# Fifty small chained transfers on the SP queue of a sliding-window kernel

## The chip, the cores and the metric

The kernel runs on one core of a Trainium2 chip. The metric is the time of one execution on the device in microseconds (us): 193.0 us, the median of three runs (192.89 to 193.47). A profiled execution has in addition a span, from its first to its last instruction; durations below come from that one execution.

The engines named here are ACT (ScalarE), DVE (VectorE), POOL (GpSimd) and SP (SyncE). SP, ACT and POOL issue DMA transfers; 16 DMA engines carry them out. In the profile the DMA queue of SP is q1, that of ACT is q10 and that of POOL is q0.

## The reference

The input `x` has 16 images of 64 channels with 64 x 64 float32 values. Windows of 8 x 8 are cut out at every fourth row and column, 15 x 15 of them, for every image and channel.

```python
n_h = (h - window_size) // stride + 1
n_w = (w - window_size) // stride + 1
for i in range(n_h):
    for j in range(n_w):
        h_start = i * stride
        w_start = j * stride
        result[:, i, j] = x[:, :, h_start:h_start + window_size, w_start:w_start + window_size].copy()
```

Nothing is computed: values are copied, each to about four places. 16.8 MB are read and 59 MB written.

## The kernel before

The whole input is held on the core in one tile `L`. A partition stands for an image, one half of the channels and one quarter of the rows (16 x 2 x 4 = 128 partitions), and holds 32 channels x 16 rows x 64 columns. Lines 49 to 54 load it in 16 transfers of 1 MB, in turn from SP and ACT, eight each. A transfer reuses one of eight completion semaphores, so the second four on each queue wait for the first four to land.

Then windows are copied out of `L` into contiguous buffers, and these are scattered to the output. The work is a list of 60 pairs (j, s), where j is the window's column (15 of them) and s the window's row within the quarter (4 of them). The function `window` does one pair, or one half of its channels. For s = 0 to 2 ACT makes the copy into a buffer `g` (line 111). For s = 3 the window reaches into the next quarter, that is into the next partition: DVE copies the upper half (line 113) and fetches the lower one with a shuffle across partitions (line 114). There are nine buffers `G0` to `G8`, each for one whole pair or two halves, used in turn.

A finished buffer is written in one of two ways:

- Usually POOL issues an indirect DMA, a scatter (line 124): each of the 128 partitions writes one contiguous row, of 8 KB for a whole pair or 4 KB for a half, to the place that an index tile names (`idx`, `idx_last`, and `idx_h`, `idx_hlast` for halves).
- For the last two pairs (`TAIL = 2`, line 115) SP issues plain stores, one for each quarter (line 118): four for the first and three for the second, 256 KB each. These seven are called the tail stores below.

The first twelve pairs (`EARLY`, line 135) begin with the first half of the channels, which has been loaded first; their second halves follow in between later pairs. Then a plain loop runs over the rest (line 146). Before the last two pairs `at` is set back by three buffers (line 148), so that they take buffers that come free early.

The order of the instructions on each engine is that of the program text. A framework adds the waits that data dependences need. The stores to `out` are declared free of dependences on each other (function `free`). On SP, therefore, the program before has eight loads and then seven tail stores, the first of which waits for an ACT copy into its buffer and the fifth for DVE's.

Of the kernel before, what the change touches and what calls it, by code (L numbers as in the profile page):

```python
# [1 line left out]

# [4 lines left out]


@with_exitstack  # L10
def kernel(
    ctx: ExitStack,
    tc: tile.TileContext,
    x: bass.AP,
    window_size: int,
    stride: int,
    out: bass.AP,
):
    nc = tc.nc
    P = nc.NUM_PARTITIONS  # L20

    B, C, H, W = x.shape
    Bo, NH, NW, Co, WSo, WSo2 = out.shape
    WS = int(window_size)
    ST = int(stride)
    assert Bo == B and Co == C and WSo == WS and WSo2 == WS

    f32 = mybir.dt.float32
    i32 = mybir.dt.int32
    ALU = mybir.AluOpType  # L30
    HQ = 4
    CH = P // (B * HQ)
    CL = C // CH
    RB = H // HQ
    NSLOT = RB // ST
    NWIN = NH * NW
    CFREE = CL * WS * WS
    assert HQ == 4 and CH == 2 and WS == 2 * ST

    lpool = ctx.enter_context(tc.tile_pool(name="lpool", bufs=1))  # L40
    ipool = ctx.enter_context(tc.tile_pool(name="ipool", bufs=1))
    gpool = ctx.enter_context(tc.tile_pool(name="gpool", bufs=1))


    L = lpool.tile([P, CL, RB, W], f32)
    x_v = x.rearrange("b (ch cl) (hq r) w -> hq (b ch) cl (r w)", ch=CH, hq=HQ)
    NCH = 4
    cw = CL // NCH
    for k in range(NCH):
        for q in range(HQ):  # L50
            (nc.sync, nc.scalar)[q % 2].dma_start(
                out=L[q::HQ, k * cw : (k + 1) * cw, :, :],
                in_=x_v[q, :, k * cw : (k + 1) * cw, :],
            )


    def itile(name):
        return ipool.tile([P, 1], i32, name=name)

    pi, tb, tq, tc_, idx, idx_last = (itile(n) for n in ("pi", "tb", "tq", "tc", "idx", "idx_last"))  # L60
    nc.gpsimd.iota(pi[:, :], pattern=[[0, 1]], base=0, channel_multiplier=1)  # L61
    nc.vector.tensor_scalar(out=tb[:, :], in0=pi[:, :], scalar1=3, scalar2=None, op0=ALU.logical_shift_right)  # L62
    nc.vector.tensor_scalar(out=tc_[:, :], in0=pi[:, :], scalar1=2, scalar2=1, op0=ALU.logical_shift_right, op1=ALU.bitwise_and)  # L63
    nc.vector.tensor_scalar(out=tq[:, :], in0=pi[:, :], scalar1=HQ - 1, scalar2=None, op0=ALU.bitwise_and)  # L64
    nc.vector.tensor_scalar(out=tb[:, :], in0=tb[:, :], scalar1=float(NWIN * CH), scalar2=None, op0=ALU.mult)  # L65
    nc.vector.tensor_tensor(out=tb[:, :], in0=tb[:, :], in1=tc_[:, :], op=ALU.add)  # L66
    nc.vector.tensor_scalar(out=tc_[:, :], in0=tq[:, :], scalar1=float(NSLOT * NW * CH), scalar2=None, op0=ALU.mult)  # L67
    nc.vector.tensor_tensor(out=idx[:, :], in0=tb[:, :], in1=tc_[:, :], op=ALU.add)  # L68

    nc.vector.tensor_scalar(out=tq[:, :], in0=tq[:, :], scalar1=float(HQ - 1), scalar2=float(2 * B * NWIN * CH), op0=ALU.is_equal, op1=ALU.mult)  # L70
    nc.vector.tensor_tensor(out=idx_last[:, :], in0=idx[:, :], in1=tq[:, :], op=ALU.add)  # L71


    HCL = CL // 2
    idx_h, idx_hlast = itile("idx_h"), itile("idx_hlast")
    for d, e in ((idx_h, idx), (idx_hlast, idx_last)):
        nc.vector.tensor_scalar(out=d[:, :], in0=e[:, :], scalar1=2.0, scalar2=None, op0=ALU.mult)  # L77
    o_v = out.rearrange("b i j (ch cl) r w -> (b i j ch) (cl r w)", ch=CH)
    o_h = out.rearrange("b i j (ch cl) r w -> (b i j ch) (cl r w)", ch=2 * CH)
    nxt = [min(p + 1, 31) for p in range(32)]  # L80

    order = [(j, s) for j in range(NW) for s in range(NSLOT)]


    TAIL, BACK = 2, 3
    o_q = out.rearrange("b i j (ch cl) r w -> i j b ch (cl r w)", ch=CH)

    def free(st):
        tc.declare_no_dep(st.ins, group="stores", reason="each store writes rows of its own")
        tc.add_to_no_dep_group("stores", st.ins)  # L90


    UNITS = 18
    G = [gpool.tile([P, 2 * HCL, WS, WS], f32, name=f"G{n}") for n in range(UNITS // 2)]
    at = 0

    def window(j, s, half):
        nonlocal at
        cols = slice(j * ST, j * ST + WS)
        last = s == NSLOT - 1  # L100
        if half is None:
            n, c0 = 2, 0
            at += at % 2
        else:
            n, c0 = 1, half * HCL
        u = at % UNITS
        at += n
        cs = slice(c0, c0 + n * HCL)
        g = G[u // 2][:, u % 2 * HCL : (u % 2 + n) * HCL, :, :]
        if not last:  # L110
            nc.scalar.copy(out=g, in_=L[:, cs, s * ST : s * ST + WS, cols])  # L111
        else:
            nc.vector.tensor_copy(out=g[:, :, 0:ST, :], in_=L[:, cs, s * ST : RB, cols])  # L113
            nc.vector.stream_shuffle(out=g[:, :, ST:WS, :], in_=L[:, cs, 0:ST, cols], mask=nxt)  # L114
        if (j, s) in order[-TAIL:]:
            g_q = g.rearrange("(m q) c r w -> q m (c r w)", q=HQ)
            for q in range(HQ - 1 if last else HQ):
                free(nc.sync.dma_start(out=o_q[q * NSLOT + s, j], in_=g_q[q]))
            return
        if half is None:  # L120
            o, ix = o_v, (idx_last if last else idx)
        else:
            o, ix = o_h, (idx_hlast if last else idx_h)
        st = nc.gpsimd.indirect_dma_start(  # L124
            out=o,
            out_offset=bass.IndirectOffsetOnAxis(ap=ix[:, 0:1], axis=0),
            in_=g.rearrange("p c r w -> p (c r w)"),
            in_offset=None,
            element_offset=(s * NW + j) * CH * CFREE + (half or 0) * HCL * WS * WS,
            bounds_check=B * NWIN * CH * (1 if half is None else 2) - 1,  # L130
            oob_is_err=False,
        )
        free(st)

    EARLY = 12
    for j, s in order[:EARLY]:
        window(j, s, 0)
    late = list(order[:EARLY])
    rest = list(order[EARLY:])
    while late:  # L140
        for w in late[:2]:
            window(*w, 1)
        for w in rest[:2]:
            window(*w, None)
        late, rest = late[2:], rest[2:]
    for w in rest[:-TAIL]:
        window(*w, None)
    at -= 2 * BACK
    for w in rest[-TAIL:]:
        window(*w, None)  # L150


# [1 line left out]
_INS = ['x', 'window_size', 'stride']  # L154
_OUTS = [((16, 15, 15, 64, 8, 8), 'float32')]

_NUMBERS = {'window_size': 8, 'stride': 4}


# [26 lines left out]
```

## Time and profile before

| What | Value |
|---|---|
| median of three runs | 193.0 us |
| profiled execution | 193.19 us |
| its span | 191.4 us |
| busy: ACT, POOL, DVE | 86.2, 68.0, 30.4 us |
| bytes moved by DMA, mean rate | 75.80 MB, 396 GB/s |
| packets: SP queue, ACT queue, POOL queue | 2512, 2176, 10080 |
| share of the 16 DMA engines: POOL, SP, ACT queue | 73.3%, 13.8%, 11.1% |
| a 1 MB load from SP, issue to landing (median) | 21.1 us |
| a scatter of a whole pair, issue to landing (median) | 18.4 us |
| a tail store of 256 KB, issue to landing (median) | 4.2 us |

Busy times count an engine's own work; issuing a DMA is not counted. The time from issue to landing of a transfer includes its wait behind others, and with several transfers of a queue under way it is far longer than the transfer itself. Where a profile's line gives packets of a queue, a packet is one contiguous row that one DMA engine moves, or a semaphore update of 4 bytes.

### The profile page before, as it was taken

The numbers are of one execution on the slowest core, as the hardware profiler recorded it, in microseconds if no ns is written. First come the engines' busy times: TensorE is split into PE (matmuls) and PEld (weight loads), VectorE is DVE, ScalarE is ACT, GpSimd is POOL, SyncE is SP. The second block draws the span as 40 slices with busy tenths as digits, with TensorE's granted clock in tenths as the row PEclk, the third lists the DMA queues.
The fourth block names the chain that finished last, engine by engine and source line by source line (L and its number), as shares of the span: only waits on it lengthen the run. The fifth ranks groups of instructions, "written<-read, shape, count | busy, mean of one in ns | idle before, by whom it ended". The sixth has DMA issues, their size and how long they took to land.

```text
span 191.4 us, 479 instructions
## 1 busy us (share of the span) xinstructions
DVE 30.4 (16%) x65; ACT 86.2 (45%) x55; POOL 68.0 (36%) x75
## 2 busy tenths in 40 slices
DVE  2000050000232302301221031203030303000030
ACT  0000059400699876364566556565647473300300
POOL 0000028723367666464464343434444444400000
DMA  5999999999999999999999999999999999999785
GB/s 180 419 413 410 410 409 413 416 423 420 417 423 429 423 418 425 407 406 414 410 413 404 414 416 413 404 409 409 411 407 409 411 409 406 416 411 416 325 265 187
DMA packets 14772, 75.80 MB, mean 396 GB/s; under 512 B 2032, under 2 KB 2032, under 8 KB 9008
## 3 DMA queue, kind: packets, MB, share of 16 engines
q0 software_dynamic: 10080, 57.15, 73.3%
q1 hardware_dynamic: 2512, 10.22, 13.8%
q10 hardware_dynamic: 2176, 8.39, 11.1%
q14 instruction: 4, 0.03, 0.0%
HBM read 16.78 MB, written 62.65 MB: 415 GB/s over the span
## 4 chain that ended last, share of the span: by engine, by line
DMA 73%; issue 19%; ACT 2%; POOL 1%; DVE 1%; POOLq 0%; DVEq 0%; PEldq 0%; ACTq 0%
DMA out_dram<-G,idx 60%; DMA out_dram<-G,idx_h 13%; ACT G L111 2%; POOL out_dram L124 1%; DVE G L114 1%; DVE G L113 0%; POOLq L124 0%; POOL pi L61 0%; DVEq L113 0%; PEldq L181 0%; ACTq L111 0%
## 5 line engine op out<-in xcount | busy, mean ns | idle before, releaser
L111 ACT COPY G<-L 128x2048 f32<-128x2048 f32 (+1 forms) x54 | 84.9, 1611 | 69.1 <-DMA out_dram<-G,idx_last 25.1
L124 POOL DMA_INDIRECT out_dram<-G,idx x35 | 33.8, 966 | 45.9 <-DMA out_dram<-G,idx 41.7
L113 DVE COPY G<-L 128x1024 f32<-128x1024 f32 (+1 forms) x18 | 11.1, 614 | 152.1 <-DMA out_dram<-G,idx 76.5
L124 POOL DMA_INDIRECT out_dram<-G,idx_h x18 | 17.4, 964 | 13.9 <-DMA out_dram<-G,idx_hlast 4.8
L114 DVE STREAM_SHUFFLE G<-L 128x1024 f32<-128x1024 f32 (+1 forms) x18 | 19.6, 1091 | 0.0
L124 POOL DMA_INDIRECT out_dram<-G,idx_hlast x6 | 5.9, 989 | 27.8 <-DVE G L114 26.3
L124 POOL DMA_INDIRECT out_dram<-G,idx_last x11 | 10.6, 964 | 10.6 <-DVE G L114 5.8
L111 ACT ACT_TABLE_LOAD x1 | 1.3, 1283 | 25.9 <-DMA L<-in_x_dram 25.9
L62 DVE TENSOR_SCALAR tb<-pi 128x1 int32<-128x1 int32 x1 | 0.2, 154 | 1.0 <-POOL pi L61 1.0
L61 POOL IOTA pi<- 128x1 int32 x1 | 0.1, 119 | 0.4 <-PEq L181 0.4
L114 DVE LOAD_MASK_SELECT G<-L x18 | 0.2, 12 | 0.0
L167 POOL MEMSET const-float32-0.0<- 128x1 f32 x1 | 0.1, 98 | 0.2 <-issue 0.2
L66 DVE CUSTOM_DVE_ANT_0 tb<-tb,tc 128x2 uint16<-128x2 uint16 x1 | 0.2, 160 | 0.0
L68 DVE CUSTOM_DVE_ANT_0 idx<-tb,tc 128x2 uint16<-128x2 uint16 x1 | 0.2, 158 | 0.0
L67 DVE TENSOR_SCALAR tc<-tq 128x1 int32<-128x1 int32 x1 | 0.2, 153 | 0.0
L77 DVE TENSOR_SCALAR idx_hlast<-idx_last 128x1 int32<-128x1 int32 x1 | 0.2, 153 | 0.0
L77 DVE TENSOR_SCALAR idx_h<-idx 128x1 int32<-128x1 int32 x1 | 0.2, 154 | 0.0
L71 DVE CUSTOM_DVE_ANT_0 idx_last<-idx,tq 128x2 uint16<-128x2 uint16 x1 | 0.2, 153 | 0.0
L65 DVE TENSOR_SCALAR tb<-tb 128x1 int32<-128x1 int32 x1 | 0.2, 151 | 0.0
L70 DVE TENSOR_SCALAR tq<-tq 128x1 int32<-128x1 int32 x1 | 0.1, 147 | 0.0
L64 DVE TENSOR_SCALAR tq<-pi 128x1 int32<-128x1 int32 x1 | 0.1, 144 | 0.0
L63 DVE TENSOR_SCALAR tc<-pi 128x1 int32<-128x1 int32 x1 | 0.1, 143 | 0.0
(3 smaller groups left out, 0.3 us busy)
## 6 DMA issues: line engine op xcount, KB each, us to landing
L<-in_x_dram SPq DMA_DIRECT2D x8, 1024.0 KB, 21.1
L<-in_x_dram ACTq DMA_DIRECT2D x8, 1024.0 KB, 19.8
out_dram<-G SPq DMA_DIRECT2D x7, 256.0 KB, 4.2
out_dram<-G,idx POOLq DMA_INDIRECT x35, 18.4
out_dram<-G,idx_h POOLq DMA_INDIRECT x18, 14.1
out_dram<-G,idx_last POOLq DMA_INDIRECT x11, 18.4
out_dram<-G,idx_hlast POOLq DMA_INDIRECT x6, 11.9
```

The source lines that it names most:

```text
L61: nc.gpsimd.iota(pi[:, :], pattern=[[0, 1]], base=0, channel_multiplier=1)
L62: nc.vector.tensor_scalar(out=tb[:, :], in0=pi[:, :], scalar1=3, scalar2=None, op0=ALU.logical_shift_right)
L65: nc.vector.tensor_scalar(out=tb[:, :], in0=tb[:, :], scalar1=float(NWIN * CH), scalar2=None, op0=ALU.mult)
L66: nc.vector.tensor_tensor(out=tb[:, :], in0=tb[:, :], in1=tc_[:, :], op=ALU.add)
L67: nc.vector.tensor_scalar(out=tc_[:, :], in0=tq[:, :], scalar1=float(NSLOT * NW * CH), scalar2=None, op0=ALU.mult)
L68: nc.vector.tensor_tensor(out=idx[:, :], in0=tb[:, :], in1=tc_[:, :], op=ALU.add)
L71: nc.vector.tensor_tensor(out=idx_last[:, :], in0=idx[:, :], in1=tq[:, :], op=ALU.add)
L77: nc.vector.tensor_scalar(out=d[:, :], in0=e[:, :], scalar1=2.0, scalar2=None, op0=ALU.mult)
L111: nc.scalar.copy(out=g, in_=L[:, cs, s * ST : s * ST + WS, cols])
L113: nc.vector.tensor_copy(out=g[:, :, 0:ST, :], in_=L[:, cs, s * ST : RB, cols])
L114: nc.vector.stream_shuffle(out=g[:, :, ST:WS, :], in_=L[:, cs, 0:ST, cols], mask=nxt)
L124: st = nc.gpsimd.indirect_dma_start(out=o, out_offset=bass.IndirectOffsetOnAxis(ap=ix[:, 0:1], axis=0), in_=g.rearrange("p c r w -> p (c r ...
```

## The change

Between the part that treats the early pairs and the loop over the rest, a tile `S` of 128 partitions x 512 B is made, in a pool of its own. Fifty transfers are then issued from SP, each the same: the first 512 B of each of the sixteen images of `x` go to sixteen partitions of `S` (32, 36, ... 92). Nothing reads `S`. Since all fifty write the same place, each one waits until the one before it has landed.

```diff
             window(*w, None)
         late, rest = late[2:], rest[2:]
+
+    spool = ctx.enter_context(tc.tile_pool(name="spool", bufs=1))
+    S = spool.tile([P, 128], f32, name="S")
+    x_s = x.rearrange("b c h w -> b (c h w)")
+    for n in range(50):
+        nc.sync.dma_start(out=S[32:93:4, :], in_=x_s[:, 0:128])
+
     for w in rest[:-TAIL]:
         window(*w, None)
     at -= 2 * BACK
```

On SP the order becomes: eight loads, the fifty transfers, seven tail stores. The instructions of ACT, DVE and POOL stay the same, in the same order.

## The prediction

> **What bounds the kernel now.** I read the 40 slices first, then the chain that ended last, then the waits of SP, then the DMA queues in short windows, and last the trace's packet records themselves (each DMA packet with queue, size, start and duration).
>
> ```profile
> DMA  5999999999999999999999999999999999999785
> ...
> GB/s 180 419 413 410 410 409 413 416 423 420 417 423 429 423 418 425 407 406 414 410 413 404 414 416 413 404 409 409 411 407 409 411 409 406 416 411 416 325 265 187
> ...
> DMA 73%; issue 19%; ACT 2%; POOL 1%; DVE 1%; POOLq 0%; DVEq 0%; PEldq 0%; ACTq 0%
> ```
>
> The 16 DMA engines are full from 5 us to about 177 us at some 412 GB/s; no compute engine is near its limit (ACT 45%). Only the last three slices, from 177 us, have slack. The kernel is bound by bytes, then by a short tail. The SP queue's own instructions and waits:
>
> ```profile
> 0.73 25.68 SPq L51 DMA_DIRECT2D L<-in_x_dram  x8
> 181.14 6.21 SPq L118 DMA_DIRECT2D out_dram<-G  x7
> ```
>
> ```profile
> SPq L118 <- ACT G L111: 154.0, 1, 154.0
> SPq L51 <- DMA L<-in_x_dram: 20.1, 4, 6.6
> ```
>
> SP issues eight loads up to 25.8 us, sleeps 154 us for the last ACT copy, and issues the seven tail stores of L118 from 181.14 us. The last of these lands at 190.4, and the span ends at 191.4. So anything put on SP has 154 us in which it delays no instruction; after that, each us of delay moves the end by a us. The price of a small transfer in a full DMA system is the whole question, so I looked at how the queues share the engines. Three queues were active between 31.6 and 34 us:
>
> ```profile
> q1 hardware_dynamic: 88, 0.36, 36.6%
> q10 hardware_dynamic: 89, 0.36, 36.3%
> q0 software_dynamic: 88, 0.29, 30.3%
> ```
>
> Columns are packets, MB, share of 16 engines. SP (q1), ACT (q10) and POOL (q0) got equal packet counts; in the packet records an engine serves them one packet each in turn. That is for queues that are already filled. A transfer that arrives new fares worse, seen at two places. First the start, between 2.2 and 4.6 us:
>
> ```profile
> q10 hardware_dynamic: 191, 0.78, 95.4%
> ...
> L<-in_x_dram SPq DMA_DIRECT2D x3, 1024.0 KB, 18.3
> L<-in_x_dram ACTq DMA_DIRECT2D x2, 1024.0 KB, 16.9
> ```
>
> SP and ACT issued their first loads together (0.735 and 0.738 us), yet ACT's packets start at 2.23 and run alone, 11 to 20 on an engine, until SP's first at 4.68 us: 2.45 us behind. Second the tail, between 182.4 and 183.3 us:
>
> ```profile
> q1 hardware_dynamic: 16, 0.13, 52.7%
> q0 software_dynamic: 21, 0.17, 45.8%
> ```
>
> The first store (issued 181.14) starts at 182.44 to 182.66 us on the eight engines that had run out of scatters. The eight still busy finish all their scatter packets (up to seven of 8 KB, 309 ns each) and start it only at 183.3 to 184.05 us, without taking turns.
>
> **What the Trainium skill says.** "DMA: Bandwidth & Descriptors", section "Queues, rings and completion order", says that each engine goes round-robin between queue rows and "drains a whole packet" of some 9 to 17 descriptors before it switches. The steady alternation above is finer than that, one 4 KB record each; the two late arrivals look more like it. The same page, "Anatomy of one DMA", prices a transfer at about 2.0 us fixed, most of it the receipt of the last write, fitted for transfers issued from GpSimd; no lone small transfer is in this trace, but the pieces below sum to 2.1 us. Its section on why a DMA increments its semaphore by 16 says that a transfer whose slowest dimension is 16 uses 16 engines, and all must have landed. The trace agrees: each tail store has 16 semaphore landings. So the slowest of 16 engines sets each step.
>
> **The change part by part.** Nothing is removed. Tile S and 50 transfers are added. In the compiled program they stand on SP between the eight loads and the seven stores; ACT, DVE and POOL keep the same instructions in the same order. All 50 write the same rows of S, so each waits for its predecessor's completion; the first eight also wait for the loads that used their semaphores before. It is a chain of round trips, not a stream.
>
> Bytes: 50 x 16 x 512 B = 0.41 MB, at 412 GB/s 1.0 us, plus 800 semaphore packets of 9 ns over 16 engines, 0.45 us. Beside the scatters about two thirds of this counts: 1 us on their end. No compute engine needs S.
>
> Start: transfer 1 is issued after SP's last load (25.8 us) and a load of ACT's that lands at 27.1. It stands in SP's queue behind four loads, the last of which lands at 49.5. So transfer 1 lands at about 49.9, and transfer 2 is issued there. From that issue to the issue of transfer 50 are 48 steps.
>
> Idle step, once the scatters are over: issue to first packet 1.30 us (181.14 to 182.44), 0.3 more for a first packet (8 KB took 616 ns there against 309 in the stream), 512 B 0.02, semaphore packet to landing 0.45 (median of 128 on SP's loads 0.49, in the tail about 0.35), landing to SP's next issue 0.02 (10.44 to 10.457): 2.1 us. Bounds 1.8 (tail values, no extra read time) to 2.4 (the first load took 1.49 us to its first packet).
>
> Loaded step: 1.30, plus the wait behind packets that the engine has already taken in, plus 0.02, plus one 8 KB scatter packet taken in turn ahead of the semaphore packet 0.31, plus 0.47, plus 0.02; without the wait that is 2.12. The wait is the unknown. If arrivals took turns at once it is at most one packet, 0 to 0.31, and the step 2.1 to 2.45. The tail gives 1.6 (184.05 less 182.44, a lower end, since the scatters ran out there). The start gives 2.45. If an engine takes in a number of packets, not of bytes, then 13 of 309 ns are 4.0. I take 2.1, which is 13 packets of 4 KB at 159 ns: the wait is then one of bytes (53 KB an engine). Loaded step 4.2 us; both ends kept: 3.4 to 6.2.
>
> Sum: the scatters end at 184.2 in the packet records, 185.5 with the added traffic. From 49.9 that is 135.6 us, 32.3 loaded steps. The remaining 15.7 take 33 us idle. Transfer 50 is issued at 218.5, the first store at 219.1. From there the tail took 10.25 us before (181.14 to 191.4); its eight busy engines are now free, so I take 9.7. Span 228.8; with the 1.8 us that the profiled execution has around its span (193.19 less 191.4) 230.6. The median of the runs shown is 193.0, 0.2 below the profiled one, inside the rounding. Forecast 231 us.
>
> By the same sum, a loaded step of 3.4 gives 215, 5.0 gives 241, 6.2 gives 252 (260 with the idle step at 2.4); the idle step at 1.8 takes 5 off the forecast. The 154 us sleep covers the chain as long as its step is below (181.14 - 0.6 - 49.9)/48 = 2.72 us: beyond that point the stores wait.
>
> **Rivals.**
> First, *deep queue*: the engine holds a count of packets, and 8 KB ones make the wait 4 us. For: 11 to 20 of ACT's packets ran before SP's first, and the records show packets, not bytes. Against: a scatter's first packet on the busy engines at 31.6 us came 3.2 us after POOL's instruction ended at 28.4, with two queues full, which leaves no room for two counts of 13. 244 to 262 us.
>
> Second, *shallow queue*: arrivals wait hardly a packet or two more than on a free engine, step 2.75 to 3.4. For: the alternation between filled queues is one for one, so a queue never waits long by turn alone. Against: both late arrivals. The first store needed 4.0 us from issue to its last landing (185.16), with a single packet more than a small transfer. 196 to 213 us.
>
> Third, *the other side, absorbed*: the step is below 2.72 us, the chain ends before 181 us in SP's sleep, and the tail starts where it did. Then only the bytes count. Where the scatters' added 1 us is taken up by the slack of the last three slices (half of the engines are done at 180.9 while the rest run to 184.2), the time stays 192.8 to 193.6, not slower; where it lands on the slow half it is 194 to 196. Speaking for it: turns one for one price the step at 2.1 to 2.45. It decides only if the wait of a new arrival is under 0.6 us.
>
> That the change doesn't do what it says: the order on SP and the waits between the 50 are in the compiled program, so I give it nothing.
>
> **How the numbers follow.** Main case (step 3.4 to 5.2) 213 to 244 us, 0.62; deep 0.15; shallow 0.13; absorbed 0.10, of which slower by bytes 0.05, no change 0.03, faster 0.02 (nothing in the profile makes it faster but a chance re-timing of the tail). About 0.3%, 0.6 us, is what a measurement of this kernel tells from no change. Range: 208 to 255 leaves out the fastest part of the shallow case, the absorbed one and the deep case's upper end, together about 0.2. Faster 0.02, same 0.03, slower 0.95.
>
> **What would show it.** SP's row: 50 transfers from 26 us, one after the other, the spacing 4.2 us to about 185 us and 2.1 us after; the stores of L118 at about 219 us, waiting for S and no longer for ACT. POOL, ACT and DVE end within 2 us of where they did. DMA slices full to 185 us, then nearly empty for over 30 us, then 4 to 5 us busy. The scatters' waits unchanged. I am wrong if the spacing beside the scatters is under 2.72 us, if it is the same before and after 185 us, or if the scatters themselves slow by more than 3 us because small packets break their stream.

## The result and the profile after

| | before | after |
|---|---|---|
| median time | 193.09 us (192.89 to 193.47, 4 runs) | 241.43 us (241.21 to 242.09, 4 runs) |
| profiled execution, its span | 193.19, 191.4 us | 241.38, 239.6 us |
| last scatter packet ends | 184.2 us | 184.3 us |
| first tail store issued | 181.1 us | 229.9 us |
| first store to the end of the span | 10.3 us | 9.7 us |

The ratio is 1.2506, 95% interval [1.2475, 1.2538]: slower by 48 us. The forecast was 231 us, slower by 38, in a range of 208 to 255.

The page of the changed kernel, its 40 slices (6 us each): share of the DMA engines and what they moved.

```profile
DMA  6999999999999999999999999999993000000045
...
GB/s 223 419 409 409 410 416 420 421 417 422 422 424 420 410 408 409 412 417 412 414 410 408 409 413 406 412 413 406 416 419 157 4 6 4 4 4 5 5 134 176
```

The copying is as fast as before and as early done. Then follow seven slices, some 42 us, in which the DMA engines move 4 to 6 GB/s, which is one small transfer at a time, and only after them the two slices of the tail stores. The same in the timeline of SP (start, duration, instructions):

```profile
0.73 25.69 SPq L51 DMA_DIRECT2D L<-in_x_dram  x8
27.11 202.77 SPq L151 DMA_DIRECT2D S<-in_x_dram  x50
229.92 4.88 SPq L118 DMA_DIRECT2D out_dram<-G  x7
```

SP's waits show what took the place of its sleep (engine, line, what it waited for: total, times, longest). Before, the tail stores waited 154 us for ACT; that row is gone, and the chain waits for itself, 49 times:

```profile
SPq L151 <- DMA S<-in_x_dram: 173.6, 49, 18.9
SPq L51 <- DMA L<-in_x_dram: 20.1, 4, 6.6
SPq L151 <- DMA L<-in_x_dram: 3.9, 2, 3.3
```

One view has to be read with care. These are two rows of the waits of the other engines:

```profile
DVE G L113 <- DMA S<-in_x_dram: 20.8, 1, 20.8
...
ACT G L111 <- DMA S<-in_x_dram: 13.8, 1, 13.8
```

They look as if DVE and ACT waited for the chain. They don't: nothing reads S. Both wait for the loads of L, and transfer 1 uses the completion semaphore of one of these loads again, so the profile puts its name there. The last load landed at 49.55 us, the two copies began at 49.65 and 49.67, and transfer 1 landed only at 49.88. Before, the same 13.8 us of ACT stood against the load.

The price of a step is read from the transfers that write S, in two windows of the changed kernel: 100 to 175 us, beside the scatters, and 187 to 205 us, with the DMA engines free.

```profile
L151 SPq DMA_DIRECT2D S<-in_x_dram x13: 492/492/493, 99.9 to 169.6; - x13
...
DMA to landing us min/median/max: 5.5/5.7/6.5
```

```profile
L151 SPq DMA_DIRECT2D S<-in_x_dram x10: 492/492/492, 186.8 to 203.4; - x10
...
DMA to landing us min/median/max: 1.8/1.8/1.9
```

From issue to landing the same 8 KB take 5.7 us beside the scatters and 1.8 us alone. A step, from one issue to the next, is hardly longer: from transfer 2, issued at 49.9 us, to transfer 26 at 184.8 there are 24 steps of 5.62 us on average; from there to transfer 50 at 229.4 another 24, of 1.86 us.

Transfer 25, issued at 180.84 us, falls between the two. At that time half of the engines run out of scatters, and the other half have scatters up to 184.3. Its sixteen packets split in the same way: eight start 1.37 to 1.49 us after the issue, as on free engines, and the other eight at 183.90 to 184.29 us, just when the last scatter packets end (183.86 to 184.28). The records name no engine, so the packets are matched by time; the same split of eight and eight is there in e3 and e12. The wait is thus one at the single engine, behind its scatters, and not one of the transfer as a whole.

### The profile page after: what moved, and what is told of

It is laid out like the page before. It is cut to its first block, busy times and chain, and to the rows that moved or that the text cites. A ratio compares the mean times of both kernels' runs of the same rounds, so it can differ in the third digit from the quotient of the medians.

```text
span 239.6 us, 534 instructions
## 1 busy us (share of the span) xinstructions
DVE 30.6 (13%) x65; ACT 86.2 (36%) x55; POOL 68.2 (28%) x75
## 4 chain that ended last, share of the span: by engine, by line
DMA 64%; ACT 5%; issue 4%; POOL 1%; SPq 1%; DVE 1%; POOLq 0%; ACTq 0%; DVEq 0%
DMA out_dram<-G,idx 48%; DMA L<-in_x_dram 9%; DMA out_dram<-G,idx_h 7%; ACT G L111 5%; POOL out_dram L124 1%; SPq L51 1%; ACT L111 1%; DVE G L114 1%; DVE G L113 0%; POOLq L124 0%; ACTq L111 0%; DVEq L113 0%
## 6 DMA issues: line engine op xcount, KB each, us to landing
out_dram<-G,idx_h POOLq DMA_INDIRECT x18, 13.8
```

## The experiments

The main theory: each new transfer waits behind what every DMA engine has already taken in from the scatters; fifty such round trips (from issue to landing) in a chain outlast SP's sleep; and the tail stores stand behind them on SP. Rivals: the cost goes by bytes or by number; it is the latency of reading device memory while it is being written; it is something that grows with the rows of a transfer.

**A shorter chain** (e1_len24).

```diff
-    for n in range(50):
+    for n in range(24):
```

> The chain cut from 50 to 24 transfers. Theory (the chain delays only the tail stores, and only after SP's sleep is used up): transfer 24 is issued at about 175 us, before the last ACT copy ends, so the stores start at 181.1 us as without a chain and the time is 193.0 to 194.3 us. Rival (each small transfer disturbs the scatters by itself): 24 of 50 transfers cost 24/50 of the 48 us, 216 us.

Measured: 193.35 us against 193.13 beside it, ratio 1.0012 [0.9998, 1.0026]. The timeline of SP in this kernel:

```profile
27.18 149.82 SPq L151 DMA_DIRECT2D S<-in_x_dram  x24
181.69 6.16 SPq L118 DMA_DIRECT2D out_dram<-G  x7
```

The 24 transfers take 150 us and cost nothing that can be measured, because SP has nothing else to do until 181 us. The rival of a fixed price for each transfer, 216 us here, falls.

**The same transfers without the chain** (e2_tiles8).

```diff
-    S = spool.tile([P, 128], f32, name="S")
+    S = [spool.tile([P, 128], f32, name=f"S{m}") for m in range(8)]
-        nc.sync.dma_start(out=S[32:93:4, :], in_=x_s[:, 0:128])
+        nc.sync.dma_start(out=S[n % 8][32:93:4, :], in_=x_s[:, 0:128])
```

> All 50 transfers stay, with the same bytes and packets, but go to eight tiles in turn, so that each waits for the eighth before it. Theory (the wait on the one before is what costs): eight round trips run side by side, 50 transfers take some 7 x 5.7 us = 40 us, end near 92 us, and the time is 193.0 to 194.5 us. Rival (fifty more transfers cost by their number or by their bytes in a full system): 235 us or more.

Measured: 194.82 us against 193.13, ratio 1.0086 [1.0054, 1.0118]. All 50 transfers with all their bytes are there, and the 48 us are not: the dependence makes them. What is left is 1.7 us, 0.3 above the expected bound; the prediction had priced bytes and turns at 1.0 to 1.45 us. The chain ended at 100 us, some 8 us later than expected, with the transfers going out every 1.43 us. The expectations of e5 and e6 below read this as a round trip of 8 x 1.43 = 11.5 us. The trace says otherwise. SP's instructions between 70 and 98 us:

```profile
L151 SPq DMA_DIRECT2D S<-in_x_dram x20: 1360/1395/1456, 69.6 to 97.0; - x20
```

The DMA instruction itself takes 1.4 us instead of 0.49, and the next one starts some 44 ns after it. SP's waits in this run have no row for S: it is never held up by the eighth transfer before. The last packet of a transfer starts some 5.9 us after its issue, against 5.03 in the chain, and long before the eighth transfer after it goes out. So the waits overlap, and what sets the pace is SP's issuing; why an instruction takes longer with some four transfers under way stays open.

**Two and three under way** (e5_tiles2, e6_tiles3): the same edit with two tiles (`n % 2`) and three (`n % 3`).

> The 50 transfers go to two tiles in turn: each waits for the second before it, two are under way. If two waits overlap fully, a pair takes 5.7 us, 2.85 each, 47 are done beside the scatters, and transfer 50 is issued at about 186: 197 us. If each transfer under way adds 0.8 us to the round trip, as eight under way (11.5 us for a round trip against 5.7 for one) suggest, a pair takes 6.5, 3.25 each, some 41 are done by 185 and the last is issued at about 191: 203 us. Rival (the engine serves one small transfer of SP's in each 5.7 us, however many are under way): 241 us.

> Three tiles in turn, three under way. By 4.9 + 0.8 us for each one under way a round trip takes 7.3 us, 2.4 us a transfer, under the 2.72 us that SP's sleep allows: the chain ends near 168 us, the stores start where they did, and only the bytes and turns are left, 194.0 to 195.2 us. Rival (depth doesn't matter or the cost goes by number): 230 us or more.

Measured: two tiles 194.27 us (one run, beside 193.39), three tiles 194.69 us, ratio 1.0072 [1.0052, 1.0092]. SP's timeline with two tiles:

```profile
27.35 155.45 SPq L151 DMA_DIRECT2D S<-in_x_dram  x50
182.85 5.05 SPq L118 DMA_DIRECT2D out_dram<-G  x7
```

My estimate that each transfer under way adds 0.8 us was wrong: transfer 3 is issued at 50.1 and transfer 50 at 182.3 us, 23.5 pairs of 5.63 us, so two waits overlap fully. I also counted a step too many, since transfers 1 and 2 both went with the loads. With two under way the chain just fits (the stores start 1.7 us later than before), and nearly the whole loss is gone. With three the last transfer is issued at 138.9 us, where I expected 168.

**Another source** (e3_from_sbuf).

```diff
-        nc.sync.dma_start(out=S[32:93:4, :], in_=x_s[:, 0:128])
+        nc.sync.dma_start(out=S[32:93:4, :], in_=L[32:93:4, 0, 0:2, :].rearrange("p r w -> p (r w)"))
```

> The 50 transfers read 512 B from sixteen partitions of L instead of from x. Theory (the extra 3.2 us of a step beside the scatters are a wait behind scatter packets that each DMA engine has already taken in): the source doesn't matter, the step stays at 5.5 to 5.9 us beside the scatters and 1.7 to 1.9 after them, 239 to 242 us. Rival (the extra is the time that a read from device memory takes while the scatters write there at full rate): the step falls to 2.3 to 2.8 us beside the scatters, the chain fits in SP's sleep, 193 to 196 us.

Measured: 236.38 us. The transfers of this kernel, 100 to 175 us and 187 to 205 us:

```profile
L150 SPq DMA_DIRECT2D S<-L x13: 486/487/487, 99.8 to 169.6; - x13
...
DMA to landing us min/median/max: 5.4/5.7/6.1
```

```profile
L150 SPq DMA_DIRECT2D S<-L x12: 486/487/487, 186.8 to 204.9; - x12
...
DMA to landing us min/median/max: 1.6/1.6/1.6
```

Between 100 and 175 us the step is the same to the hundredth, 5.74 us on average in both kernels; alone it is 0.2 us shorter, which over the 24 idle steps makes the 5 us of difference. (The time lies 2.6 us under the range that I had expected; the idle step of 1.64 us lay just under mine.) Reading device memory is not what makes the loaded step long.

**One row instead of sixteen** (e8_one_row).

```diff
-        nc.sync.dma_start(out=S[32:93:4, :], in_=x_s[:, 0:128])
+        nc.sync.dma_start(out=S[32:33, :], in_=x_s[0:1, 0:128])
```

> Each of the 50 transfers moves one row of 512 B only, on one DMA engine instead of sixteen. Theory (the step is set by the slowest of sixteen engines, each with about the same wait): the median engine's packet came 0.3 us before the last one's beside the scatters and 0.1 us after them, so the step falls to 5.2 to 5.5 us and 1.65 to 1.8 us, 236 to 240 us. Rival (the step's excess grows with the number of engines or rows[...]): under 4 us beside the scatters, under 225 us.

Measured: 220.37 us; the step is 4.96 us beside the scatters (100 to 175 us) and 1.21 alone. SP's instruction, from 100 to 175 us:

```profile
L151 SPq DMA_DIRECT2D S<-in_x_dram x15: 202/202/203, 103.1 to 172.7; - x15
```

The packet records split the time from the issue to the start of the 512 B packet:

| mean | issue to packet, scatters | issue to packet, alone | difference |
|---|---|---|---|
| sixteen rows, median engine | 4.76 us | 1.39 us | 3.37 us |
| one row | 4.31 us | 0.86 us | 3.45 us |

Both sides were off. The rival had named under 225 us, and the time is there, but the loaded step is not under 4 us, and what the scatters add is the same with one engine as with sixteen. What does grow with the rows is the fixed part, which I had expected to fall by 0.1 to 0.2 us and which fell by 0.6. About half of that is the DMA instruction itself, which takes 202 ns on SP for one row and 492 ns for sixteen.

**Is it packets or bytes?** (e4_half_rows, e9 to e11.) First all scatters in halves:

```diff
     for w in rest[:-TAIL]:
-        window(*w, None)
+        window(*w, 0)
+        window(*w, 1)
```

(and the same for the pairs between the late halves).

> All scatters go out as halves, so that their packets are 4 KB and not 8 KB; twice as many, the same bytes. The wait of a new transfer behind scatter packets was 3.25 us with 8 KB packets (10.5 of them). If an engine takes in a fixed number of packets: wait 1.7, step 3.5 to 4.0 us. If it takes in a fixed number of bytes: wait 3.25, step 5.3 to 5.6. If it is between, as steps 2 and 3 of the chain beside 4 KB packets suggest (2.6): step 4.6 to 5.0 us. The time follows from the step, from about 222 (3.8) over 234 (4.8) to 240 us (5.5), if POOL keeps the queue filled with twice as many scatters.

Measured: 223.29 us. The time is no answer, as POOL couldn't keep the queue filled with twice as many scatters: the last scatter packet ended at 197.9 us, not at 184.3. The kernel in windows (after the window's length: busy of DVE, ACT, POOL; clock; DMA share; GB/s):

```profile
50.00:100.00 50.00, 11.82 (x33) 38.27 (x39) 34.89 (x36) 1.00 1.00 400
100.00:150.00 50.00, 10.71 (x30) 28.19 (x27) 33.55 (x34) 1.00 0.91 354
150.00:180.00 30.00, 4.35 (x12) 13.57 (x13) 22.07 (x23) 1.00 0.88 343
```

Where the share falls to 0.9 the step falls to 3.19 us on average (32 steps from 88 us on): a little slack in the queues takes 2.5 us off. But from 59 to 83 us the queue was still full, every scatter packet had 4 KB, and four transfers came then. Their packets took 4.82 us from issue on the median engine, 3.43 over the idle 1.39 (3.2 to 3.9 in the four). Beside 8 KB packets it was 3.37. Divided by a packet's median time, that is some 22 packets of one kind (159 ns each) and 11 of the other (314 ns), and 88 KB of both. A fixed count of 11 packets would have waited 1.7 us here; these four rule it out.

Then the start of the program, where POOL loads L and the chain runs beside it: all loads on POOL, the chain moved ahead, the rows of a load cut by `PIECES` = 1, 2, 4 (with `NK` = 4, 2, 1, so that a load stays at 1 MB).

```diff
+    for k in range(NK):
+        for g in range(PIECES):
+            for q in range(HQ):
+                nc.gpsimd.dma_start(
+                    out=L[q::HQ, ck * k : ck * k + ck, rk * g : rk * g + rk, :],
+                    in_=x_v[q, :, ck * k : ck * k + ck, rk * W * g : rk * W * (g + 1)],
+                )
```

> All sixteen loads of L go on POOL's queue, in packets of 4 KB, and the chain starts on SP beside them, at the start of the program. In the first 40 us each transfer of the chain arrives while every engine has loads of POOL's queued. Wait of its first packet (time from issue, less the 1.28 us of an idle system): if an engine takes in bytes (some 53 to 84 KB), 2.1 to 3.3 us; if it takes in 10 to 13 packets, 1.6 to 2.1 us. This run is the base for the next two.

> The same with the loads in packets of 2 KB, the same bytes in each load. Bytes: the wait stays within 0.4 us of that beside 4 KB packets. Count: it falls to about half of it, some 0.8 to 1.1 us.

> The same with the loads in packets of 1 KB. Bytes: the wait stays within 0.6 us of that beside 4 KB packets (more if such packets move slower). Count: about a quarter of it, some 0.4 to 0.6 us.

Measured: 221.99, 226.76 and 228.07 us; the times also hold the slower loads and the rest of the chain. What was asked for is the wait from 14 to 36 us. From issue to landing, rows of 4 KB (e9):

```profile
DMA to landing us min/median/max: 4.7/4.7/4.8
```

Rows of 2 KB (e10):

```profile
DMA to landing us min/median/max: 5.0/5.0/5.0
```

Rows of 1 KB (e11):

```profile
DMA to landing us min/median/max: 5.3/5.4/5.4
```

The wait doesn't fall with shorter rows; it rises about as much as the loads slow down. On the median engine it is 2.54, 2.74 and 3.09 us over the idle 1.39, with the loads at 411, 388 and 348 GB/s. Times a sixteenth of that rate: 65, 66 and 67 KB. With one reservation: the records show packets of 4 KB in all three, several short rows in one, so these runs vary the rows and the rate and not the packet. They can't tell 66 KB from 16 packets of 4 KB; only the halves above can. Taken together bytes fit and a fixed count does not, but it is not one number of bytes: some 66 KB an engine of loads, some 88 KB of scatters. Why scatters have more of it stays open.

**Another engine for the stores** (e7_stores_on_act).

```diff
-                free(nc.sync.dma_start(out=o_q[q * NSLOT + s, j], in_=g_q[q]))
+                free(nc.scalar.dma_start(out=o_q[q * NSLOT + s, j], in_=g_q[q]))
```

> The seven tail stores are issued by ACT, the chain of 50 stays on SP. Theory (the 48 us are the chain's length plus the stores queued behind it): the stores land by 191 us, the end is the landing of transfer 50 at 231 us, span 232 and time 234 us, so that 7 to 8 of the 48 us go and the rest is the chain itself. Rival (the order on SP alone makes it late, not the chain's length): 193 to 196 us.

Measured: 235.54 us, near the expected 234, since the chain ended at 231 us as forecast. But the stores did not land by 191 us. In the timeline of ACT:

```profile
179.64 1.90 ACT L111 COPY G<-L 128x2048 f32<-128x2048 f32 x1 [14.48 <-DMA out_dram<-G,idx_last]
...
217.53 12.21 ACTq L118 DMA_DIRECT2D out_dram<-G  x7
```

The stores were free of SP's queue and still started 36 us after the copy. In the trace, SP and ACT share eight completion semaphores, used in turn. The first store gets the one of transfer 43 and has to wait for it: transfer 43 was issued at 215.67 us and landed at 217.5. The six others follow transfers 44 to 49 one by one, each within 0.1 us of the landing. So moving the stores to another queue does not free them from the chain here, and how much of the loss is their place behind it on SP was not measured.

**A chain in between** (e12_len32): 32 transfers.

> The chain cut to 32 transfers. By the changed kernel's steps, transfers 2 to 25 take 5.6 us beside the scatters and each later one 1.86: 18 fewer of these, 241.4 - 18 x 1.86 = 208 us, within 1.5. Rival (the cost goes by the number of transfers, 48.3/50 each): 224 us.

Measured: 206.73 us, 1.3 below the 208 of the steps and 17 below the rival's 224. The timeline of SP:

```profile
27.18 169.14 SPq L151 DMA_DIRECT2D S<-in_x_dram  x32
196.36 4.48 SPq L118 DMA_DIRECT2D out_dram<-G  x7
```

By these runs transfers cost nothing measurable up to 24 (e1). Between 32 and 50 they cost a little under 2 us each: (241.43 - 206.73) / 18 is 1.93, and the steps themselves 1.86. The rest is in the tail, which from the first store to the end of the span took 8.5 us here and 9.7 with 50 transfers.

None of the runs is faster than the kernel before.

## Why the prediction was right, and what it had wrong

**Bound and mechanism**: right. The bytes end at 184.3 us as before (184.2), SP's 154 us sleep is used up by the chain (50 transfers against 24, e1 and the changed kernel), and each us after that moves the end (e12). The chain is what costs, not the bytes: with all 50 transfers but more of them under way, 0.9 to 1.7 us are left (e2, e5, e6). I had taken 1 us for bytes and turns; how much of what is left is theirs was not separated, and in e5 later stores are part of it.

**The loaded step** is the term that was mis-sized, and in it the wait:

| term | taken | measured |
|---|---|---|
| issue to first packet, free engines | 1.30 us | 1.28 us |
| wait behind what is taken in, over that | 2.1 us | 3.5 us median engine, 3.75 slowest |
| scatter packet ahead of the semaphore's | 0.31 us | 0.33 us |
| semaphore packet to landing, next issue | 0.49 us | 0.4 us |
| loaded step | 4.2 us | 5.7 us |
| idle step | 2.1 us | 1.86 us |

(The waits of 3.4 us above are over 1.39 us, the median engine's idle time; here they are over the first packet's 1.28.) I had three views of the wait: 1.6 us from the tail, which I myself called a lower end, 2.45 from the start, and 4.0 if packets are counted. I took 2.1, below the only view with a full queue, by pricing 13 packets of 4 KB at 159 ns; beside the loads of e9 the wait is 16 of them. And I carried bytes from loads to scatters, which hold a third more. That the wait goes by bytes rather than by a count of packets fits e4; the deep-queue rival, which counted packets, falls, though its 4.0 us was nearer to the slowest engine's 3.75 than my figure.

**The sum**: 24 loaded steps instead of 32.3, so 24 idle ones instead of 15.7. That is 8.3 more at 1.86 us, 15 us; the idle step being 0.24 shorter (0.3 us from the semaphore packet to landing, where I had taken 0.45, is the larger part) gives 4 back, and the end of the loaded steps at 184.8 instead of 185.5 us 1 more. Together 11 us: transfer 50 was issued at 229.4, not 218.5. The tail's 9.7 us and the 1.8 us around the span came as taken. The measured step lies outside the 3.4 to 5.2 us of my main case, and 5.62 put into the sum as it stood gives 248 us. That the time still fell into the main case's 213 to 244 is luck: the idle step erred the other way and took some 6 us off.

**The Trainium skill's** 2.0 us fixed for a transfer, in "DMA: Bandwidth & Descriptors", section "Anatomy of one DMA", was fitted for transfers issued from GpSimd. It comes near to a lone one of SP's with sixteen rows, 1.86 us; one row took 1.21, well below it. The page puts most of it into the receipt of the last write; here 1.39 of the 1.86 us pass before the median packet starts. Beside full queues the measured 5.7 us decides. The same page's section "Why a DMA increments its semaphore by 16 and not by 1", from which I said that the slowest engine sets the step, fits in size: the last of the sixteen packets starts 5.03 us after the issue, the median one 4.76.

**The other rivals**: *shallow queue* needed a step of 2.75 to 3.4 us; such a step appeared only in e4, once the scatters no longer filled the queue. *Absorbed* happened with 24 transfers and with two, three or eight under way, and cost 0.2 to 1.7 us there.

## What to carry to other kernels

A small transfer beside full DMA queues costs a round trip of nearly 6 us here against under 2 alone; ask of each such transfer whether the next one waits for it, and give it a second buffer: two in turn took away 47 of the 48 us. Compare the chain's length with the sleep of the queue that it runs on, and see what stands behind it there, not with the DMA engines' share of busy time. Look also at which completion semaphores later transfers share with it: an engine of its own was not enough.

## What was not expected of the hardware

- A newly arriving transfer of another queue waits as long as an engine needs for some 66 KB of loads (2.54 us, e9) or 88 KB of scatters (3.37 us, changed kernel), by my estimate from the wait and the rate, though filled queues are served one packet each in turn (31.6 to 34 us before). That the engine took these bytes in beforehand is the reading that fits; the records show only the order.
- The step beside the scatters is the same for reads of device memory and of the core's own memory (5.74 us); alone they differ by 0.2 us (e3).
- SP's DMA instruction took 202 ns for one row (e8) and 492 ns for sixteen; issued back to back beside the scatters, the same sixteen rows took 1.4 us (e2).
- Loads on POOL's queue in rows of 2 KB and 1 KB show as packets of 4 KB, of 173 and 192 ns against 164 (medians, 14 to 36 us, e9 to e11).
- A DMA share of 0.9 in place of 1.0 brought the step from 5.9 to 3.2 us (e4).
